# One value matmul for the high and low parts of the attention probabilities, with the second half of the bank copied by ScalarE and added by GpSimd

## The chip, the cores and the metric

The kernel runs on one core of a Trainium2 chip. The metric is the time of one execution on the device in microseconds (us). The kernel before takes 2233.69 us, the median of three runs (2232.92 to 2233.96).

Engines are named as in the profile: PE is the matrix engine (TensorE) and PEld its weight loads, DVE is VectorE, ACT is ScalarE, POOL is GpSimd, SP is the engine that issues the transfers. Each executes its own instructions in a fixed order and waits for others by semaphores.

## The reference

The reference is one layer of a decoder: a SwiGLU half block, two attention mixers side by side, a second SwiGLU half block and a gated input embedding, for 1024 tokens of width 1024 in float32. The change is inside the two mixers. Each has 8 heads of width 64:

```python
# forgetting attention, per block of queries
logits = jnp.einsum('bqhd,bkhd->bhqk', qi, k) * scale
logits = logits + Fq[..., None] - Fk          # running sums of log forget gates
w = jax.nn.softmax(jnp.where(mask, logits, -jnp.inf), axis=-1)
y = jnp.einsum('bhqk,bkhd->bqhd', w, v)

# stick-breaking attention, per block of queries (strictly causal)
z = jnp.einsum('bqhd,bkhd->bhqk', qi, k) * scale
log_1m = jnp.where(mask, jax.nn.log_sigmoid(-z), 0.0)
after = lax.cumsum(log_1m, axis=3, reverse=True) - log_1m
a = jnp.where(mask, jnp.exp(jax.nn.log_sigmoid(z) + after), 0.0)
y = jnp.einsum('bhqk,bkhd->bqhd', a, v)
```

In both, a triangular matrix of probabilities is multiplied with the values of the head. The change concerns this last product.

## The kernel before

Float32 accuracy is had from two rounded parts: a tensor is split into a high part (a cast to the matrix engine's rounded format, on ACT) and a low part (what the cast left over, on DVE or POOL), and products are made part by part. For the values, both parts of a head lie side by side in one weight tile of 128 columns: columns 0 to 63 hold the high part, 64 to 127 the low part (`v2[:, kb, hd, :]`, tile X). A product of that weight with probabilities therefore gives 128 rows: rows 0 to 63 are the high values' share, rows 64 to 127 the low values' share, and the two are added afterwards.

**Steps.** The attention loop runs over 16 heads, h = 0 to 7 forgetting and h = 8 to 15 stick-breaking, and in each over four blocks c = 0 to 3 of 256 queries. One such pair (h, c) is a step here. Block c sees the keys 0 to 256(c+1). `scores` of a step makes the two rows of its probabilities (row 0 and row 1, 128 queries each) in two T tiles, in the forgetting heads so: POOL adds the mask to the bias on the diagonal block (L981), PE makes the products (L990, L991), DVE adds the bias and takes the minimum (L995, first the part left of the diagonal, which reads the bias tile GF, then the diagonal, which reads what L981 wrote), ACT takes the exponential (L1001), DVE the reciprocal (L1002) and POOL scales (L1003). In the stick-breaking heads ACT takes two sigmoids (L998, L999), POOL masks the diagonal (L1005), DVE scans (L966) and POOL multiplies (L1013, L1017). There are four T buffers, so a step reuses the two tiles of the step before last.

`apply` works on the step before: for each pair of key blocks, from the diagonal pair down, PE turns the probabilities (transposes, L1042), ACT casts the high part (L1044), DVE makes the low part (L1045) into a tile PT with the two parts side by side (`pt[:, 0, :]` and `pt[:, 1, :]`), and PE multiplies with the values (L1065). The products of all pairs are summed in one bank `av` of the accumulator memory (PSUM), of which there is one buffer. At the end ACT copies rows 64 to 127 (L1084) and DVE adds rows 0 to 63 to them (L1085), which gives 64 rows of the tile Y for this head. In the diagonal pair the second key block meets only the second 128 queries, so there the widths are 256, 128, 128, 256; in other pairs four times 256. A group here is the value matmuls of one pair; there are 160, of which 64 are diagonal.

**What sets the order.** While a step's scores and products wait for other engines, PE works on fill: other matmuls of the layer (queries, keys and values of later heads, gates, branches), a share of which is woven in after every piece by `take`. The fill has work for other engines too: ACT casts weights (L136), POOL subtracts to get their low part (L146), and for a later pair of heads POOL takes a power (L850) and scales (L852) to normalise queries and keys. PE's order is written out by hand (`pe`), as is that of the L146 among themselves and, in the stick-breaking heads, that of the scans and of L1044 and L1045. The rest is ordered by a scheduler when the program is built. Some transposes of the fill (L882) use the `av` bank too.

## Time and profile before

| | |
|---|---|
| median of three runs | 2233.69 us |
| span of the profiled execution | 2230.9 us |
| PE busy | 2218.2 us (99%) |
| DVE, ACT, POOL busy | 1490.2, 972.1, 813.9 us |
| granted PE clock | 1.00 throughout |
| forgetting heads | about 733 to 1005 us |
| stick-breaking heads | about 1005 to 1372 us |
| value matmuls (L1065) | 640 |

The profile is of one execution, the runs of three others; the span runs from the first to the last instruction, and the profiled execution has no other time of its own. A row of a group reads: line, engine, operation, output<-input, shapes, count | busy us, mean ns of one | idle time before it and what ended it. A row of the timeline reads: start, length, engine, line, operation, shapes, count (rows that follow each other alike are merged), and in brackets the engine's idle time before it. The end of a matmul is modelled, and matmuls overlap, so the distance between the starts is what one costs.

### The profile page before, as it was taken

Reading aid. Unit: us, or ns where it says so; the run is one execution under the profiler, and the core shown is the slowest. Engines: PE = TensorE matmul, PEld = TensorE weight load, DVE = VectorE, ACT = ScalarE, POOL = GpSimd, SP = SyncE. Lnnn points to the kernel's source line nnn. Section 1 sums busy time; section 2 is a strip of 40 time slices with the busy share of each in tenths; the row PEclk is TensorE's granted clock in tenths of the full one; section 3 lists DMA queues with packets and bytes.
Section 4 is the critical chain, followed back from the end, with each engine's and each line's share of the span. In section 5 each row is a group of like instructions: output and inputs, shape, how many; then the busy total and the mean of one; then the engine's idle time right before and its main releaser. Section 6 shows DMA issues by size and latency. Waiting matters only on the chain.

```text
span 2230.9 us, 29212 instructions
## 1 busy us (share of the span) xinstructions
PE 2218.2 (99%) x10857; PEld 1864.3 (84%) x10857; DVE 1490.2 (67%) x2188; ACT 972.1 (44%) x1694; POOL 813.9 (36%) x709
## 2 busy tenths in 40 slices
PE   9999999999999999999999999999999999999999
PEld 7888888888889888888988888887888888888887
DVE  7855545497895565666666676799654555778873
ACT  6433333333454555555456564245333333434441
POOL 0344444310015466455456654400644443200111
PEclk9999999999999999999999999999999999999999
DMA  8232322474433133132124236731423232655132
GB/s 325 94 121 84 112 101 98 152 291 149 147 132 96 29 95 95 29 98 69 39 72 118 62 125 215 266 140 55 140 95 118 85 128 81 254 199 208 62 119 89
DMA packets 187710, 278.03 MB, mean 125 GB/s; under 512 B 27944, under 2 KB 110120, under 8 KB 187568
## 3 DMA queue, kind: packets, MB, share of 16 engines
q1 hardware_dynamic: 187568, 276.17, 36.7%
q8 instruction: 85, 1.39, 0.3%
q14 instruction: 57, 0.47, 0.1%
HBM read 192.47 MB, written 75.27 MB: 120 GB/s over the span
## 4 chain that ended last, share of the span: by engine, by line
PE 91%; DVE 4%; ACT 2%; issue 1%; DMA 1%; POOL 0%; SPq 0%; DVEq 0%; ACTq 0%; POOLq 0%
PE ps L496 36%; PE ps L388 19%; PE ps L763 11%; PE ps L755 7%; PE ps L1307 4%; PE ps L1662 4%; PE ps L1065 3%; PE ps L1042 2%; PE ps L449 2%; PE ps L991 1%; PE ps L990 1%; PE ps L1357 1%; DVE H L113 1%; ACT H L112 1%; ACT T L1001 0%
## 5 line engine op out<-in xcount | busy, mean ns | idle before, releaser
L388 PE MATMUL ps<-H,H 128*128 128x512 f32 x2184 | 497.3, 389 | 0.0
L388 PEld LDWEIGHTS ps<-H,H 128*128 128x128 f32 x2184 | 409.5, 188 | 85.0
L496 PE MATMUL ps<-H,WL 128*128 128x512 f32 x1008 | 238.9, 389 | 0.0
L496 PEld LDWEIGHTS ps<-H,WL 128*128 128x128 f32 x1008 | 189.2, 188 | 39.3
L763 PE MATMUL ps<-H,WH 128*128 128x512 f32 x640 | 176.1, 401 | 0.0
L1045 DVE TENSOR_TENSOR PT<-ps,PT 128x512 fp32r<-128x512 f32 (+1 forms) x160 | 100.6, 634 | 78.5 <-ACT PT L1044 77.6
L496 PE MATMUL ps<-H,Q 128*128 128x512 f32 x576 | 137.4, 389 | 0.0
L396 DVE SCALAR_TENSOR_TENSOR X<-ps,X 128x512 f32<-128x512 f32 x168 | 108.6, 682 | 41.8 <-PE ps L388 41.7
L763 PEld LDWEIGHTS ps<-H,WH 128*128 128x128 f32 x640 | 113.5, 188 | 18.4
L496 PEld LDWEIGHTS ps<-H,Q 128*128 128x128 f32 x576 | 108.1, 188 | 22.5
L1044 ACT CAST PT<-ps 128x512 fp32r<-128x512 f32 (+1 forms) x160 | 86.9, 549 | 85.0 <-PE ps L1042 81.1
L146 POOL TENSOR_TENSOR WL<-RAW,WH 128x512 fp32r<-128x512 f32 (+1 forms) x92 | 108.6, 1202 | 39.4 <-ACT WH L136 28.0
L496 PE MATMUL ps<-X,WL 128*128 128x512 f32 x480 | 115.6, 390 | 0.0
L209 POOL TENSOR_TENSOR PT<-PT,RN 128x1024 f32<-128x1024 f32 x2 | 4.8, 2413 | 295.0 <-ACT RN L203 295.0
L1065 PEld LDWEIGHTS ps<-PT,X 128*128 128x128 f32 x640 | 96.7, 189 | 18.9 <-DVE PT L1045 4.7
L755 PE MATMUL ps<-WH,H 128*128 128x256 f32 (+2 forms) x576 | 111.4, 323 | 0.2 <-DVE log_f L818 0.2
L1065 PE MATMUL ps<-PT,X 128*128 128x256 f32 (+1 forms) x640 | 105.7, 283 | 2.7 <-DVE PT L1045 1.4
L496 PEld LDWEIGHTS ps<-X,WL 128*128 128x128 f32 x480 | 89.9, 188 | 19.1 <-DVE WL L113 0.5
L1003 POOL TENSOR_TENSOR T<-T,l 128x128 f32<-128x128 f32 (+3 forms) x64 | 73.2, 1150 | 88.9 <-DVE l L1002 83.6
L496 PE MATMUL ps<-H,PT 128*128 128x512 f32 x432 | 103.2, 390 | 0.2 <-DVE PT L113 0.2
L283 POOL TENSOR_TENSOR PT<-GF,RN 128x512 f32<-128x512 f32 x20 | 33.2, 1658 | 174.1 <-DVE GF L539 89.9
L496 PEld LDWEIGHTS ps<-H,PT 128*128 128x128 f32 x432 | 80.8, 188 | 18.0 <-DVE PT L113 1.3
(418 smaller groups left out, 4810.8 us busy)
## 6 DMA issues: line engine op xcount, KB each, us to landing
hidden<-PT SPq DMA_DIRECT2D x40, 512.0 KB, 3.1
WH<-in_ffn_w_gate_dram SPq DMA_DIRECT2D x38, 512.0 KB, 5.4
Q<-hidden SPq DMA_DIRECT2D x24, 512.0 KB, 6.4
hidden<-RN SPq DMA_DIRECT2D x22, 512.0 KB, 2.6
KH<-in_ffn_w_up_dram SPq DMA_DIRECT2D x20, 512.0 KB, 6.2
KL<-in_ffn_w_up_dram SPq DMA_DIRECT2D x20, 512.0 KB, 6.9
T<-in_ffn_w_down_dram SPq DMA_DIRECT2D x20, 512.0 KB, 4.4
RAW<-in_w_in_dram SPq DMA_DIRECT2D x18, 512.0 KB, 4.3
```

The costliest lines, as they stand in the source:

```text
L146: ins = eng_lo.tensor_sub(lo[part], raw[part], f(hi[part]))
L388: pe(nc.tensor.matmul(groups[g][t][:], wt[:, b, k, t * P:(t + 1) * P], act[:, a, k, :], start=(fresh and n == 0), stop=(i in (6, 1, 4) and ...
L396: nc.vector.scalar_tensor_tensor(xs, groups[g][t][:], scale, xs, ALU.mult, ALU.add)
L496: pe(nc.tensor.matmul(ps[:], hl[:, a, k, :], rhs(m, b, k), start=(first and i == 0), stop=(final and i == 11), skip_group_check=True))
L755: pe(nc.tensor.matmul(ps[:, :n], hT[t // 4][a][:, k, (t % 4) * P:(t % 4 + 1) * P], w[k // d][b][:, k % d, :n], start=(i == 0), stop=(i == ...
L763: pe(nc.tensor.matmul(ps[:], w[a][:, k, :], hT[half][b][:, k, :], start=(i == 0), stop=(i == 23)))
L1003: nc.gpsimd.tensor_mul(T[:, :n], T[:, :n], l[:].broadcast_to([P, n]))
L1044: high = nc.scalar.copy(pt[:, 0, :width], ps[:, :width])
L1045: low = nc.vector.tensor_sub(pt[:, 1, :width], ps[:, :width], f(pt[:, 0, :width]))
L1065: pe(nc.tensor.matmul(o, lh, r, start=(kpair == c and i == 0), stop=(kpair == 0 and i == 3)))
L1307: pe(nc.tensor.matmul(ps[:], w[a][:, k, :], yT[g][b][:, k, half * 512:half * 512 + 512], start=(i == 0), stop=(i == 11)))
L1662: pe(nc.tensor.matmul(ps, pl["w"][d, k // 2][b][:, k % 2, m * P:(m + 1) * P], hT[half][a][:, k, cs], start=(i == 0), stop=(i == 23)))
```

## The change

Two matmuls in place of four make a pair's product. The moving operand of one is the high and the low part of the turned probabilities, twice 256 columns, and its output takes the whole bank of 512 columns: columns 0 to 255 hold the products of the high part, 256 to 511 those of the low part. For the second key block of the diagonal pair it is twice 128. So at the end of a step the bank has four quarters. The first two (rows 64 to 127 and 0 to 63 of the first half) are joined as before. Of the second half only rows 0 to 63 are used: ACT copies them to `part` (64x256), and POOL adds `part` to Y. The product of the low values with the low probabilities (rows 64 to 127), which was in the sum before, is left out of it. `part` lies in the second T tile of the step that is being finished.

```diff
         def values(kpair):
             pt = pts[kpair]
-            mm = []
-            for kb in (2 * kpair, 2 * kpair + 1):
-                for b in range(2):
-                    c0 = (kb % 2) * 256
-                    if kb < 2 * c + 1:
-                        mm.append((av[:, 0:256], v2[:, kb, hd, :], pt[:, b, c0:c0 + 256]))
-                    else:
-                        mm.append((av[:, P:256], v2[:, kb, hd, :], pt[:, b, c0:c0 + P]))
-            if kpair == c:
-                mm = [mm[0], mm[2], mm[3], mm[1]]
-            for i, (o, lh, r) in enumerate(mm):
-                pe(nc.tensor.matmul(o, lh, r, start=(kpair == c and i == 0), stop=(kpair == 0 and i == 3)))
+            both = av[:].rearrange("p (b n) -> p b n", b=2)
+            for i in range(2):
+                kb, c0 = 2 * kpair + i, 256 * i
+                q0 = 0 if kb < 2 * c + 1 else P
+                pe(nc.tensor.matmul(both[:, :, q0:256], v2[:, kb, hd, :], pt[:, :, c0:c0 + 256 - q0], start=(kpair == c and i == 0), stop=(kpair == 0 and i == 1)))
...
         ys = Y["t"][hh * HD:(hh + 1) * HD, c * 256:(c + 1) * 256]
+        part = step["pr"][1][hh * HD:(hh + 1) * HD, 0:256]
         nc.scalar.copy(ys, av[HD:P, :256])
         nc.vector.tensor_add(ys, av[0:HD, :256], ys)
+        nc.scalar.copy(part, av[0:HD, 256:512])
+        nc.gpsimd.tensor_add(ys, ys, part)
```

In the changed kernel the value matmul is L1058, the first copy and the DVE add are L1078 and L1079, the new copy and the POOL add L1080 and L1081; all lines above these are as before.

How the change moves instructions is shown at three places. The first is PE at a diagonal pair, its value matmuls and the transposes behind them; before:

```order
L1065 MATMUL ps_9228<-PT_9233,X_7472 128x256
L1065 MATMUL ps_9228<-PT_9233,X_7472 128x128 x2
L1065 MATMUL ps_9228<-PT_9233,X_7472 128x256
L1042 MATMUL ps_9262<-identf,T_9077 128x128
L1042 MATMUL ps_9262<-identf,T_9101 128x128
```

and now:

```order
L1058 MATMUL ps_9244<-PT_9249,X_7424 128x512
L1058 MATMUL ps_9244<-PT_9249,X_7424 128x2x128
L1042 MATMUL ps_9284<-identf,T_9082 128x128
L1042 MATMUL ps_9284<-identf,T_9106 128x128
L1042 MATMUL ps_9284<-identf,T_9082 128x128
```

Four matmuls have become two; everything else on PE keeps its place.

The second place is POOL in the steps (2,0) and (2,1), the first two of the third forgetting head; before:

```order
L981 TENSOR_TENSOR T_6316<-GF_5924,mask_fox 128x128
L981 TENSOR_TENSOR T_6339<-GF_5924,mask_fox 128x128
L850 TENSOR_TENSOR qkss_5592<-qkss_5592,mhalf 128x16
L852 TENSOR_TENSOR RN_5590<-RN_5590,qkss_5592 128x1024
L1003 TENSOR_TENSOR T_6316<-T_6316,l_6318 128x128
L1003 TENSOR_TENSOR T_6339<-T_6339,l_6341 128x256
L981 TENSOR_TENSOR T_6453<-GF_5924,mask_fox 128x128
L981 TENSOR_TENSOR T_6470<-GF_5924,mask_fox 128x128
L146 TENSOR_TENSOR WL_6426<-RAW_6327,WH_6424 128x512 x2
L146 TENSOR_TENSOR WL_6431<-RAW_6330,WH_6429 128x512 x2
```

and now:

```order
L981 TENSOR_TENSOR T_6298<-GF_5918,mask_fox 128x128
L1081 TENSOR_TENSOR Y_5575<-Y_5575,T_6116 64x256
L850 TENSOR_TENSOR qkss_5592<-qkss_5592,mhalf 128x16
L981 TENSOR_TENSOR T_6321<-GF_5918,mask_fox 128x128
L852 TENSOR_TENSOR RN_5590<-RN_5590,qkss_5592 128x1024
L1003 TENSOR_TENSOR T_6298<-T_6298,l_6300 128x128
L1003 TENSOR_TENSOR T_6321<-T_6321,l_6323 128x256
L981 TENSOR_TENSOR T_6429<-GF_5918,mask_fox 128x128
L146 TENSOR_TENSOR WL_6404<-RAW_6309,WH_6402 128x512 x2
L146 TENSOR_TENSOR WL_6409<-RAW_6312,WH_6407 128x512 x2
L1081 TENSOR_TENSOR Y_5575<-Y_5575,T_6215 64x256
L981 TENSOR_TENSOR T_6446<-GF_5918,mask_fox 128x128
```

The two L981 of a step stood next to each other ahead of the fill's POOL work. Now that of row 1 stands behind the add, and with it behind L850 in (2,0) and behind four L146 in (2,1).

The third place is POOL in the step (3,0); before:

```order
L146 TENSOR_TENSOR WL_6737<-RAW_6598,WH_6735 128x512 x2
L981 TENSOR_TENSOR T_6796<-GF_6314,mask_fox 128x128
L981 TENSOR_TENSOR T_6817<-GF_6314,mask_fox 128x128
L850 TENSOR_TENSOR qkss_6507<-qkss_6507,mhalf 128x16
L852 TENSOR_TENSOR RN_6505<-RN_6505,qkss_6507 128x1024
L1003 TENSOR_TENSOR T_6796<-T_6796,l_6798 128x128
```

and now:

```order
L981 TENSOR_TENSOR T_6766<-GF_6296,mask_fox 128x128
L146 TENSOR_TENSOR WL_6711<-RAW_6574,WH_6709 128x512 x2
L850 TENSOR_TENSOR qkss_6483<-qkss_6483,mhalf 128x16
L852 TENSOR_TENSOR RN_6481<-RN_6481,qkss_6483 128x1024
L1081 TENSOR_TENSOR Y_6295<-Y_6295,T_6532 64x256
L981 TENSOR_TENSOR T_6787<-GF_6296,mask_fox 128x128
L1003 TENSOR_TENSOR T_6766<-T_6766,l_6768 128x128
```

Here the add and the L981 of row 1 stand behind both L850 and L852. On DVE the order is unchanged: the L995 of row 1 stands ahead of the first L1045 of the step, as it did.

## The prediction

> **What bounds the kernel now.** I read the page's busy times and chain of waits first, then the stretches, the groups of instructions, and the timeline round the ends of the attention steps.

> ```profile
> span 2230.9 us, 29212 instructions
> PE 2218.2 (99%) x10857; PEld 1864.3 (84%) x10857; DVE 1490.2 (67%) x2188; ACT 972.1 (44%) x1694; POOL 813.9 (36%) x709
> PE 91%; DVE 4%; ACT 2%; issue 1%; DMA 1%; POOL 0%; SPq 0%; DVEq 0%; ACTq 0%; POOLq 0%
> ...
> 733.00:1005.00 272.00, 270.07 (x1589) 234.67 (x1588) 164.30 (x507) 148.49 (x319) 151.73 (x154) 1.00 0.25 69
> 1005.00:1372.00 367.00, 365.42 (x2058) 315.95 (x2057) 246.39 (x377) 209.72 (x433) 208.46 (x227) 1.00 0.32 95
> ```

> PE is busy 99% of the span and carries 91% of the chain. The last two rows are the stretches that the change touches, forgetting heads and then stick-breaking heads (length, then busy time of PE, weight loads, DVE, ACT, POOL, and the granted clock 1.00). PE stands idle under 2 us in each. So PE time removed comes off the end, and any new PE wait goes onto it: there is no idle time to swallow it. POOL is 56% busy in the first stretch, but what counts is what stands ahead of a given instruction in its queue.

> **The matmuls.** These groups and timeline rows price them.

> ```profile
> L1065 PE MATMUL ps<-PT,X 128*128 128x256 f32 x512 | 102.4, 290 | 1.9 <-DVE PT L1045 1.1 <-ACT PT L1044 0.6
> L1065 PE MATMUL ps<-PT,X 128*128 128x128 f32 x128 | 24.2, 255 | 0.8 <-DVE PT L1045 0.2
> ...
> 793.43 0.62 PE L755 MATMUL ps<-RAW,H 128*128 128x512 f32 x2
> 793.89 0.64 PE L1065 MATMUL ps<-PT,X 128*128 128x256 f32 x4
> ...
> 799.75 0.62 PE L1065 MATMUL ps<-PT,X 128*128 128x256 f32 x4
> 800.21 0.60 PE L1042 MATMUL ps<-identf,T 128*128 128x128 f32 x4
> ...
> 839.26 0.64 PE L1065 MATMUL ps<-PT,X 128*128 128x256 f32 x4
> 839.74 0.60 PE L1042 MATMUL ps<-identf,T 128*128 128x128 f32 x4
> ```

> Since matmuls overlap, I take the distance between starts. Two 512-column matmuls take 793.89 - 793.43 = 0.46, 0.23 each. A full group (four of 256) takes 0.48, 0.12 each. A diagonal group (256, 128, 128, 256) takes 0.46 as well, so a 128-column one costs (0.46 - 0.24)/2 = 0.11, nearly as much as 256: below 256 columns it is no longer the columns that set the pace. After the change a full group is 2 x 0.23 = 0.46 and a diagonal one 0.23 + 0.12 = 0.35. The 640 matmuls are 160 groups, 64 diagonal and 96 full: 64 x 0.11 + 96 x 0.015 = 8.5 us at most.

> A matmul now reads high and low part at once, so the group cannot start on the high part while DVE finishes the low one. Comparing the start of each L1065 group with the end of its L1045, 23 of the 160 start before it. Those lose most of the gain, and full ones some 0.1 us each beside it: I take **-5.4 us** (-8.5 to -3). That the moving operand is now two runs of 256 rather than one is shown by no row; it is bounded by 0 and by the four-matmul price, a gain of 0.

> [...]

> **The new copy and add.** Each of the 64 steps gets an ACT copy of 64x256 and a POOL add of 64x256.

> ```profile
> L1084 ACT COPY Y<-ps 64x256 f32<-64x256 f32 x64 | 23.6, 369 | 71.8 <-PE ps L1065 70.7
> L1085 DVE TENSOR_TENSOR Y<-ps,Y 64x256 f32<-64x256 f32 x64 | 26.6, 415 | 47.2 <-ACT Y L1084 45.9
> L1003 POOL TENSOR_TENSOR T<-T,l 128x256 f32<-128x256 f32 x7 | 4.3, 617 | 0.1
> L1017 POOL TENSOR_TENSOR T<-T,RN 128x256 f32<-128x256 f32 x16 | 12.9, 806 | 0.0
> L1013 POOL TENSOR_TENSOR T<-T,RN 128x255 f32<-128x255 f32 x16 | 15.3, 955 | 19.2 <-DVE RN L966 19.1
> L981 POOL TENSOR_TENSOR T<-GF,mask_fox 128x128 f32<-128x128 f32 x60 | 26.5, 463 | 16.9 <-PE ps L1042 16.0 <-POOL T L1003 0.8
> L850 POOL TENSOR_TENSOR qkss<-qkss,mhalf 128x16 f32<-128x16 f32 x6 | 17.5, 2914 | 18.8 <-DVE qkss L849 18.6
> L852 POOL TENSOR_TENSOR RN<-RN,qkss 128x1024 f32<-128x1024 f32 x6 | 11.4, 1907 | 0.5
> L882 PE MATMUL ps<-identf,RN 128*128 128x128 f32 x56 | 8.5, 273 | 0.5 <-DVE Y L1085 0.5
> ```

> The copy is the L1084 copy, 0.37. The add has two full operands of 256 columns like L1017, 0.81; with a broadcast operand it would be 0.62, beside DVE scans 0.96. I take 0.81. Both engines have the time (64 x 0.81 = 52 us on POOL over 639). What counts is order: `part` lies in the second T tile of the step just applied, so that tile comes free after the POOL add and no longer after its last transpose. The next user, row 1 of the step being scored, waits: L981 on POOL, the first L995 on DVE, L998/L999 on ACT. DVE and ACT run in order, and behind the stalled L995 or L1001 stand L1044 and L1045 of the same step, which the value matmuls need.

> The order listing shows that in the forgetting heads the add often stands behind long POOL work. Worked in full for step (3,0), where it stands behind L850 and L852:

> ```profile
> 833.04 2.91 POOL L850 TENSOR_TENSOR qkss<-qkss,mhalf 128x16 f32<-128x16 f32 x1
> 834.55 0.35 DVE L995 CUSTOM_DVE_ANT_0 T<-T,ps,m 128x128 f32<-128x128 f32 x1
> 834.94 0.51 ACT L1001 ACTIVATE T<-T,m 128x256 f32<-128x256 f32 x1 [0.93 <-DVE m L995]
> 835.57 0.48 ACT L1044 CAST PT<-ps 128x384 fp32r<-128x384 f32 x1
> 836.03 1.91 POOL L852 TENSOR_TENSOR RN<-RN,qkss 128x1024 f32<-128x1024 f32 x1
> 836.08 0.56 DVE L1045 TENSOR_TENSOR PT<-ps,PT 128x384 fp32r<-128x384 f32 x1 [0.34 <-ACT PT L1044]
> 837.28 0.63 PE L1065 MATMUL ps<-PT,X 128*128 128x256 f32 x4
> ```

> L852 ends at 837.94, the add at 838.75, L981 (0.46) at 839.2. The diagonal L995 starts at 839.25 for 834.55, 4.7 late. L1001, L1044 and L1045 follow each other without slack, so the low part is ready at 836.64 + 4.7 = 841.35, and the value matmuls of 837.28 stall **4.1 us**.

> Two other patterns: in (2,0) the add comes in time but L981 stands behind L850; in (2,1) the add stands behind four L146.

> ```profile
> 794.96 0.42 DVE L1085 TENSOR_TENSOR Y<-ps,Y 64x256 f32<-64x256 f32 x1
> 796.20 2.91 POOL L850 TENSOR_TENSOR qkss<-qkss,mhalf 128x16 f32<-128x16 f32 x1 [3.24 <-DVE qkss L849]
> 796.72 0.35 DVE L995 CUSTOM_DVE_ANT_0 T<-T,ps,m 128x128 f32<-128x128 f32 x1
> 798.10 0.56 DVE L1045 TENSOR_TENSOR PT<-ps,PT 128x384 fp32r<-128x384 f32 x1 [0.20 <-ACT PT L1044]
> ...
> 805.36 5.05 POOL L146 TENSOR_TENSOR WL<-RAW,WH 128x512 fp32r<-128x512 f32 x4 [1.41 <-ACT WH L136]
> 808.55 0.55 DVE L995 CUSTOM_DVE_ANT_0 T<-GF,ps 128x384 f32<-128x384 f32 x1 [0.35 <-PE ps L991]
> 811.01 0.56 DVE L1045 TENSOR_TENSOR PT<-ps,PT 128x384 fp32r<-128x384 f32 x1 [0.34 <-ACT PT L1044]
> 811.57 0.63 PE L1065 MATMUL ps<-PT,X 128*128 128x256 f32 x4
> ```

> (2,0): L1085 ends at 795.38, the part copy some 0.6 later (L845 stands ahead of it on ACT), so add at 796.0 to 796.8, L850 to 799.7, L981 to 800.2; L995 3.5 late, the low part at 798.66 + 3.5 = 802.15 against a group at 799.75: **2.4 us**. (2,1): L146 ends at 810.41, add at 811.2; L995 2.7 late, no slack at 811.57: **2.7 us**. The same arithmetic on the other forgetting steps gives about 2.4 in (5,0), (6,0) and (3,2), 2.8 in (6,1), 1.9 in (7,0), 1.5 in (7,3), 1.4 in (3,3) and (6,2), 1.2 in (4,0), 0.6 in (7,2), 0.4 in (1,1) and (5,1), 0.3 in (3,1), nothing elsewhere: **+28 us** in all; with an add of 0.62 it is 25, of 0.96 it is 31. After a stall POOL's backlog could be shorter, since PE then starts the next step later: if every second stall of a run of neighbours vanished, 20 would be left.

> Stick-breaking heads: there the add stands behind row 0's work only.

> ```profile
> 1237.67 0.40 ACT L999 ACTIVATE T<-ps 128x256 f32<-128x256 f32 x1
> 1238.05 0.46 POOL L1013 TENSOR_TENSOR T<-T,RN 128x127 f32<-128x127 f32 x1
> 1238.90 0.28 PE L1065 MATMUL ps<-PT,X 128*128 128x256 f32 x1
> ```

> In (13,0) the add ends at 1238.51 + 0.8 = 1239.3; L999 of row 1, which stood at 1237.67, is 1.7 late, with L1044 behind it and a group at 1238.90 that has no slack: 1.7 us. Over these heads the same sum gives **+4 us** (3 to 5).

> The `av` bank comes free after the part copy, 0.37 later. L882 is the only one that already waits there (0.5 us now); at four places its slack is under 0.37: **+1 us**. SP only loses a few places in its order; its next Y store waits for one more add, and nothing waits for that. The very last add lies beside some 11 us of branch matmuls.

> Sum: 2230.9 - 5.4 + 28 + 4 + 1 = 2258.5 of span. The median of the runs (2233.69) is 2.8 above the span, so about **2260 us**.

> [...]

> **Rivals.**

> 1. *Forecast: POOL's queue decides*, 2245 to 2277. For it: PE's idle share and the three worked steps.
> 2. *No change.* The scheduler's positions hold, but the queue is short when the add arrives; then each step has only the chain copy, add, copy, POOL add. The same arithmetic with an idle POOL gives about +4 over the forgetting heads; with -5.4 + 4 + 1 that is about the same as before, near 2234. Against it: L850 alone takes 2.9 us.
> 3. *Faster.* The slack covers the lateness entirely: 119 of the 160 groups have over 0.4 us between the end of L1045 and the group's start. PE's gain stands alone, -5.4 to -8.5: 2225 to 2228. It decides if the part copy and add end before row 1's first L995, 1 to 3 us after the step's last value matmul. In about half of the steps they do; it would have to be nearly all.
> 4. *Worse.* The L146 that stand behind an add come late as well and the fill matmuls wait for their weights: 0.81 in each of some 15 steps, +12, about 2272. Or two runs of 256 cost as much as four matmuls, and the gain is nil: +5, 2265. Against both: none of the PE rows above waits for POOL now, and weights are split a step or more ahead of their use.

> **Chances.** 1: 0.62. 4: 0.20. 2: 0.10. 3: 0.08. A change within 0.2% (4.5 us) cannot be told from none here. Faster 0.08, same 0.10, slower 0.82. The range takes case 1, most of case 4 and the upper edge of 2: 2236 to 2277; the forecast's own is 2245 to 2277.

> **What would show it.** 256 value matmuls of 512 columns and 64 of 2x128, groups of 0.46 and 0.35 between starts; POOL adds near 0.8; the stretch of the forgetting heads longer by 20 to 28 us at the same PE work, with PE's idle time charged to L1045 and L1044, most in (3,0) and heads 2, 3, 5, 6 and 7; DVE's L995 or POOL's L981 waiting for POOL. Wrong would be: PE idle still under 5 us in both stretches, or a stall at steps where POOL was free.

## The result, and the profile after

The changed kernel takes 2274.88 us (median of four runs, 2274.28 to 2275.44) against 2233.38 us in the runs beside it: 1.0186 times as long, 95% interval 1.0171 to 1.0200. It is slower by 41.5 us, where 26 were forecast. The profile is of the execution of 2275.44 us.

The page of the changed kernel, first its span, PE's busy row and the chain of waits:

```profile
span 2273.7 us, 28587 instructions
PE 2228.6 (98%) x10537; PEld 1851.2 (81%) x10537; DVE 1497.4 (66%) x2188; ACT 990.8 (44%) x1758; POOL 864.4 (38%) x773
PE 82%; DVE 7%; ACT 4%; POOL 3%; issue 3%; DMA 1%; SPq 0%; POOLq 0%; DVEq 0%; ACTq 0%
```

PE's part of the chain fell from 91% to 82%, and POOL, which had none, has 3%. PE has 320 matmuls fewer and is nevertheless busy 10 us longer (2228.6 against 2218.2). That is the first sign of something the prediction had not reckoned with.

The two stretches of attention (length, then busy time of PE, weight loads, DVE, ACT, POOL, then the granted clock):

```profile
734.00:1037.00 303.00, 278.73 (x1442) 232.18 (x1442) 163.62 (x505) 155.05 (x344) 171.98 (x180) 0.96 0.23 62
1037.00:1413.30 376.30, 363.48 (x1872) 302.47 (x1871) 251.35 (x375) 220.03 (x466) 237.60 (x261) 1.00 0.31 91
```

The forgetting heads take 32 us longer (303 for 271), the stick-breaking heads 11 us (376 for 365); the rest of the program is as before to 0.2 us. PE is idle 24 us in the first stretch and 13 in the second, 1.9 and 1.6 before. And the granted clock of the first stretch is 0.96.

The matmuls, the new copy and the POOL add, by groups:

```profile
L1058 PE MATMUL ps<-PT,X 128*128 128x512 f32 x256 | 91.9, 420 | 35.7 <-DVE PT L1045 35.3
L1058 PE MATMUL ps<-PT,X 128*128 128x256 f32 x64 | 18.7, 292 | 0.0
L1081 POOL TENSOR_TENSOR Y<-Y,T 64x256 f32<-64x256 f32 x64 | 51.1, 799 | 70.5 <-ACT T L1080 61.0 <-PE ps L755 5.6 <-PE ps L763 2.4
L1080 ACT COPY T<-ps 64x256 f32<-64x256 f32 x64 | 23.4, 365 | 23.1 <-DVE Y L1079 22.5
```

The add takes 0.80 us, the copy 0.37, as estimated. PE's idle time stands almost wholly ahead of L1058, charged to the low part, L1045. Why L1045 is late the list of waits says (who waited for whom: us in total, times, longest):

```profile
DVE T L995 <- POOL Y L1081: 22.3, 16, 4.2
ACT T L999 <- POOL Y L1081: 16.0, 17, 2.9
DVE T L995 <- POOL T L981: 12.2, 8, 3.1
```

Row 1 of the scores waits for its T tile, on DVE in the forgetting heads and on ACT in the others. A step's name here is that of the step being scored; its value matmuls are those of the step before. The timeline of (3,0), which the prediction worked out in full:

```profile
839.97 2.91 POOL L850 TENSOR_TENSOR qkss<-qkss,mhalf 128x16 f32<-128x16 f32 x1 [0.48 <-DVE qkss L849]
842.96 1.90 POOL L852 TENSOR_TENSOR RN<-RN,qkss 128x1024 f32<-128x1024 f32 x1
844.82 0.71 POOL L1081 TENSOR_TENSOR Y<-Y,T 64x256 f32<-64x256 f32 x1
845.57 0.29 DVE L995 CUSTOM_DVE_ANT_0 T<-GF,ps 128x128 f32<-128x128 f32 x1 [4.24 <-POOL Y L1081]
845.62 0.45 POOL L981 TENSOR_TENSOR T<-GF,mask_fox 128x128 f32<-128x128 f32 x1
847.49 0.56 DVE L1045 TENSOR_TENSOR PT<-ps,PT 128x384 fp32r<-128x384 f32 x1 [0.20 <-ACT PT L1044]
848.10 0.62 PE L1058 MATMUL ps<-PT,X 128*128 128x512 f32 x2 [3.43 <-DVE PT L1045]
```

L850, L852, the add, L981, then DVE, ACT, DVE and at last PE, which has stood idle for 3.43 us. The chain is the predicted one, link by link; 4.1 us was the estimate. What comes behind it was not predicted. Four stretches of one us, the second and third just after this stall:

```profile
847.00:848.00 1.00, 0.00 (x0) 0.00 (x0) 0.67 (x3) 1.00 (x5) 0.61 (x1) 1.00 0.02 8
...
850.00:851.00 1.00, 1.00 (x6) 0.90 (x5) 0.50 (x1) 0.00 (x0) 0.00 (x0) 0.50 0.06 16
851.00:852.00 1.00, 1.00 (x6) 0.80 (x5) 0.00 (x0) 0.00 (x0) 0.00 (x0) 0.50 0.00 0
...
853.00:854.00 1.00, 1.00 (x9) 0.96 (x8) 0.97 (x2) 0.65 (x2) 0.00 (x0) 1.00 0.00 0
```

While PE stands idle the clock still reads 1.00 here. Some 1.5 us after it has started again the granted clock falls to 0.50, where PE has 6 matmuls in a stretch of one us for 9 behind it; after 3.41 us it is 1.00 again. There are seven such drops, after the stalls of 2.33, 3.43, 2.75, 2.13, 2.41, 3.93 and 2.44 us; six last 3.41 us and the one after 2.75 twice that. The stall of 2.43 us at 800.5 was followed by none, nor were those of 1.75 and 1.39.

What sets the one of 2.43 us apart shows in the places of the drops. They start at 818.83, 849.55, 870.03, 941.71, 982.67, 999.74 and 1276.22 us, and all the distances are whole multiples of 3.413 us (9, 6, 21, 12, 5 and 81 of them). So in this trace the drops lie on a beat of 3.413 us that does not start anew with a stall. Cut along this beat, the stalls of 2.43 us (the first three rows) and of 2.33 us (the last two) look like this:

```profile
798.35:801.76 3.41, 2.14 (x12) 1.44 (x10) 0.36 (x2) 0.45 (x2) 3.41 (x3) 1.00 0.00 0
801.76:805.18 3.42, 2.26 (x15) 2.00 (x16) 1.90 (x4) 1.59 (x5) 1.91 (x3) 1.00 0.02 5
805.18:808.59 3.41, 3.41 (x19) 2.65 (x17) 1.90 (x4) 3.15 (x5) 0.53 (x2) 1.00 0.17 38
...
815.42:818.83 3.41, 1.51 (x10) 1.47 (x11) 1.92 (x8) 1.55 (x4) 1.97 (x3) 1.00 1.01 295
818.83:822.24 3.41, 3.41 (x16) 3.41 (x15) 1.44 (x8) 2.51 (x5) 1.18 (x2) 0.50 0.60 228
```

The first stall lies across two beats, in which PE is idle for 1.27 and 1.16 us, and the next beat is at full clock. The second puts 1.90 us of idleness into one beat, and the next is at half clock. The other six drops follow beats with 1.96 to 3.41 us of idleness; among the beats without a drop behind them the largest idleness is 1.75 us.

The run of the matmuls alone (below) has the same 10537 PE matmuls in the same order and no drop before the program's end. Against its distances from start to start, the drops of the change cost **12.7 us**. By an estimate from their length, eight beats at half clock are 13.6 us of full-speed work (8 x 3.41 / 2), but at the start of three of them PE was still idle (0.68, 0.08 and 0.39 us). The four runs had a mean clock of 0.994 to 0.996; one beat at half clock takes 0.0008 off that mean (1.7 of 2274 us), so by this estimate not all had the same number of drops.

### The profile page after: what moved, and what is told of

It reads as the page before. It is cut to its first block, busy times and chain, and to the rows that moved or that the text cites. A ratio compares the mean times of both kernels' runs of the same rounds, so it can differ in the third digit from the quotient of the medians.

```text
span 2273.7 us, 28587 instructions
## 1 busy us (share of the span) xinstructions
PE 2228.6 (98%) x10537; PEld 1851.2 (81%) x10537; DVE 1497.4 (66%) x2188; ACT 990.8 (44%) x1758; POOL 864.4 (38%) x773
## 4 chain that ended last, share of the span: by engine, by line
PE 82%; DVE 7%; ACT 4%; POOL 3%; issue 3%; DMA 1%; SPq 0%; POOLq 0%; DVEq 0%; ACTq 0%
PE ps L496 35%; PE ps L388 18%; PE ps L763 6%; PE ps L755 6%; PE ps L1658 4%; PE ps L1303 3%; PE ps L1058 3%; PE ps L449 2%; PE ps L1042 2%; POOL WL L146 1%; PE ps L1353 1%; PE ps L991 1%; PE ps L990 1%; DVE PT L1045 1%; DVE H L113 1%
## 5 line engine op out<-in xcount | busy, mean ns | idle before, releaser
L1045 DVE TENSOR_TENSOR PT<-ps,PT 128x512 fp32r<-128x512 f32 (+1 forms) x160 | 100.0, 633 | 73.0 <-ACT PT L1044 72.1
L1058 PE MATMUL ps<-PT,X 128*128 128x512 f32 x320 | 99.9, 394 | 35.7 <-DVE PT L1045 35.3
L146 POOL TENSOR_TENSOR WL<-RAW,WH 128x512 fp32r<-128x512 f32 (+1 forms) x92 | 104.9, 1161 | 37.3 <-ACT WH L136 32.7
L1044 ACT CAST PT<-ps 128x512 fp32r<-128x512 f32 (+1 forms) x160 | 85.5, 546 | 67.2 <-PE ps L1042 66.2
L755 PE MATMUL ps<-WH,H 128*128 128x256 f32 (+2 forms) x576 | 112.0, 325 | 0.2 <-DVE log_f L818 0.2
L1058 PEld LDWEIGHTS ps<-PT,X 128*128 128x128 f32 x320 | 56.4, 193 | 62.1 <-DVE PT L1045 54.1
L966 DVE TENSOR_TENSOR_SCAN RN<-GF,RN 128x127 f32<-128x127 f32 (+2 forms) x96 | 96.6, 1007 | 2.8
```

Source lines behind the costliest of these rows:

```text
L146: ins = eng_lo.tensor_sub(lo[part], raw[part], f(hi[part]))
L755: pe(nc.tensor.matmul(ps[:, :n], hT[t // 4][a][:, k, (t % 4) * P:(t % 4 + 1) * P], w[k // d][b][:, k % d, :n], start=(i == 0), stop=(i == ...
L966: order("dve", nc.vector.tensor_tensor_scan(*args))
L1044: high = nc.scalar.copy(pt[:, 0, :width], ps[:, :width])
L1045: low = nc.vector.tensor_sub(pt[:, 1, :width], ps[:, :width], f(pt[:, 0, :width]))
L1058: pe(nc.tensor.matmul(both[:, :, q0:256], v2[:, kb, hd, :], pt[:, :, c0:c0 + 256 - q0], start=(kpair == c and i == 0), stop=(kpair == 0 an ...
```

## The experiments

The theory after the result: the T tile, held past its transposes for the new part, makes row 1 of the next scores late; POOL's queue turns that into stalls of microseconds; and long stalls cost clock on top (the tile theory). Two rivals: the merged matmul stalls for its own sake, because it needs the low part before it can start (the matmul theory); or the added work on ACT and POOL makes both late in whatever buffer the part lies (the load theory). Each median stands beside that of runs of the kernel before on the same chip; those medians are 2233.05 to 2233.26 us.

### The matmuls alone

```diff
-        part = step["pr"][1][hh * HD:(hh + 1) * HD, 0:256]
         nc.scalar.copy(ys, av[HD:P, :256])
         nc.vector.tensor_add(ys, av[0:HD, :256], ys)
-        nc.scalar.copy(part, av[0:HD, 256:512])
-        nc.gpsimd.tensor_add(ys, ys, part)
```

> The two matmuls per pair alone: neither the new copy nor the POOL add is made, so the share of the low probabilities is left out of the result. This prices the matmul side by itself. Tile and load theory: 4 to 8 us faster than before, 2225 to 2229 us, granted clock 1.00 throughout. Matmul theory: 2260 to 2275.

Measured: 2229.84 us, 0.9986 of before (0.9976 to 0.9995), 0.8 us above what the tile and the load theory gave. Its busy times, and behind them what PE waited for (us in total, times, longest):

```profile
PE 2211.3 (99%) x10537; PEld 1842.0 (83%) x10537; DVE 1489.1 (67%) x2188; ACT 971.5 (44%) x1694; POOL 813.7 (37%) x709
...
PE ps L1058 <- DVE PT L1045: 6.4, 15, 1.2
PE ps L882 <- DVE Y L1078: 1.9, 2, 1.4
```

The matmul theory falls: the merge makes the kernel 3.2 us faster. PE's idle time in attention rose from 3.5 to 8.9 us, so the matmuls themselves save 8.6 us (3.2 + 5.4), the 8.5 of the prediction's upper bound, and waits for the low part take most of it back.

### The copy and the add alone

```diff
+        part = step["pr"][1][hh * HD:(hh + 1) * HD, 0:256]
+        nc.scalar.copy(part, av[0:HD, 0:256])
+        nc.gpsimd.tensor_add(ys, ys, part)
```

added to the kernel before, with its four matmuls.

> The four matmuls of before, and beside them the new copy and POOL add with the part in the T tile (the part is copied from rows 0 to 63 of the first half, so those are added twice). Tile theory: all the cost and none of the gain, 2265 to 2282 us. Matmul theory: 2232 to 2238, as before. Load theory: 2255 to 2275.

Measured: 2276.56 us, 1.0194 of before (1.0178 to 1.0210): the whole loss, without the merged matmul, as the tile theory had it and 1.6 us above the upper end of the load theory. Its value matmuls now wait, where they had waited for 2.7 us in all:

```profile
L1065 PE MATMUL ps<-PT,X 128*128 128x256 f32 x512 | 106.9, 298 | 23.7 <-ACT PT L1044 21.5 <-DVE PT L1045 1.9
```

Here PE waits for the high part instead of the low one, since this group may start on the high part. Both stand behind row 1 in their queues, which fits the loss being much the same. The granted clock is 0.96 in the forgetting heads (734 to 1037 us) and 1.00 in the others, as with the change.

### The part in a buffer of its own

```diff
-        part = step["pr"][1][hh * HD:(hh + 1) * HD, 0:256]
+        part = stat([P, 256], "part", 1)[hh * HD:(hh + 1) * HD, :]
```

and, to make room, the size 1088 of the buffers RAW, WH, WL and Y set to 1056.

> The part lies in a buffer of its own (64x256, one buffer) and no longer in the step's second T tile; copy, POOL add and matmuls stay. Tile theory (T comes free only behind the POOL add, so row 1 of the next scores is late, PE stalls, and long stalls cost clock): the 33 us of added PE idle and the 14 us of clock go, 2226 to 2236 us. Matmul theory (a group of two matmuls cannot start before the low part and stalls by itself): 2265 to 2275, as the whole change. Load theory (52 us more on POOL and 23 us more on ACT make both late, in whatever buffer): 2250 to 2270.

Measured: 2251.71 us (1.0081; 1.0063 to 1.0100). That is 16 us above the tile theory's upper end and inside what the load theory gave, although the clock is 1.00. But the stretches tell of another cause: before and behind attention, where no instruction was changed, it takes 4.7 and 7.7 us longer. One group of the first 700 us shows it, before and here:

```profile
L496 PE MATMUL ps<-H,WL 128*128 128x512 f32 x504 | 119.4, 389 | 0.0
```

```profile
L496 PE MATMUL ps<-H,WL 128*128 128x512 f32 x504 | 121.7, 393 | 0.0
```

These matmuls take their weights from a WL tile. Such matmuls became slower with the new size and make up 9 of the 12 us (sums of the distances between starts, against the run of the matmuls alone); the rest is spread over others, by under 1 us each. So 12 us of this run are the buffers' layout, and the next run leaves the layout as it was. Its part is rounded to bfloat16, which takes half the bytes:

```diff
-        part = step["pr"][1][hh * HD:(hh + 1) * HD, 0:256]
+        part = st.tile([P, 256], mybir.dt.bfloat16, tag="part", bufs=1, name=nm("part"))[hh * HD:(hh + 1) * HD, :]
```

> Copy and POOL add as in the change, the part in a buffer of its own that fits without making other buffers smaller (bfloat16, 512 bytes a partition). In e1_own the stretches outside attention, where nothing was changed but buffer sizes, were 12 us longer; here they should be as before, 734 and 856 us. Tile theory: 2231 to 2238 us. Load theory: 2245 to 2255.

Measured: 2239.54 us, 1.0030 of before (1.0018 to 1.0041), between the two forecasts and nearer to the tile theory. Up to the first value matmul and from the last one on it takes 734.1 and 860.8 us, as before (734.2 and 860.8). The profile is of the fastest of its six executions, 2237.21 us, without a clock drop; the slowest, 2241.60 us, had a mean clock of 0.998. Inside attention:

```profile
734.00:1006.60 272.60, 266.26 (x1443) 223.48 (x1442) 163.62 (x506) 156.28 (x344) 169.35 (x180) 1.00 0.25 69
1006.60:1375.00 368.40, 360.88 (x1873) 301.45 (x1872) 249.54 (x375) 219.69 (x466) 237.52 (x260) 1.00 0.32 94
```

In the forgetting heads (first row) PE is idle 6.3 us, as with the matmuls alone: there the tile explains the whole loss. In the stick-breaking heads it is idle 7.5 us against 2.7 with the matmuls alone and 12.8 with the change. So there the load theory has its share: some 4.8 us come from the copy on ACT and the add on POOL although the tile is free, 5.3 from the tile. The one buffer is not what costs instead: no copy into it waits for the add before. Which of copy and add makes the 4.8 us was not taken apart.

### The tile or POOL's add

```diff
-        nc.gpsimd.tensor_add(ys, ys, part)
+        nc.vector.tensor_add(ys, ys, part)
```

> The change, but the last add on DVE and not on POOL; the part still lies in the T tile. This separates POOL's queue from the tile. If the queue is the cause (the add and L981 stand behind L850, L852 and L146), the tile comes free about 1.3 us after the first DVE add, which most steps can bear: 2231 to 2240 us, clock 1.00. If holding the T tile past its transposes is enough by itself: 2250 to 2275.

Measured: 2258.46 us, 1.0114 of before (1.0099 to 1.0130). Neither forecast named the mechanism, which the timeline of step (3,0) shows:

```profile
836.73 0.42 DVE L1081 TENSOR_TENSOR Y<-Y,T 64x256 f32<-64x256 f32 x1 [0.28 <-ACT T L1080]
836.80 3.12 POOL L850 TENSOR_TENSOR qkss<-qkss,mhalf 128x16 f32<-128x16 f32 x1
840.00 1.90 POOL L852 TENSOR_TENSOR RN<-RN,qkss 128x1024 f32<-128x1024 f32 x1
841.86 0.45 POOL L981 TENSOR_TENSOR T<-GF,mask_fox 128x128 f32<-128x128 f32 x1
842.35 0.35 DVE L995 CUSTOM_DVE_ANT_0 T<-T,ps,m 128x128 f32<-128x128 f32 x1 [4.76 <-POOL T L981]
844.41 1.01 PE L1058 MATMUL ps<-PT,X 128*128 128x512 f32 x2 [3.63 <-DVE PT L1045]
```

The last add is now done by DVE in good time, at 837.15. But L981, the mask add of row 1, can only start after it, and L850 and L852 now stand ahead of it in POOL's order. PE stalls for 3.63 us without any new instruction on POOL. So the forgetting heads stall without an add on POOL too: PE is idle there for 19.6 us, against 24.3 with the change and 6.3 with the matmuls alone. That the tile is held some microseconds past its transposes, and L981 has thereby lost its place ahead of the fill's POOL work, is enough for most of it. The added DVE work is not the cause: with a second DVE add and no tile held (under "Versions without the tile") PE is idle there for 9.0 us. With the add on POOL it is worse by 16 us, since the add too waits in that queue: PE is idle for 9.6 us more in both stretches together, and eight beats run at half clock instead of four.

If so, it must help to give L981 its place back and keep tile, copy and POOL add. In the next version both mask adds of a forgetting step are issued first and the waiting L850 and L852 (`norm`) behind them. The POOL add then no longer stands behind L850 and L852 either, so this run does not tell the two apart; the one before does.

```diff
+            for i in (2 * step["c"], 2 * step["c"] + 1):
+                Ts[i] = slot("T", [P, S])
+                mask = nc.gpsimd.tensor_add(Ts[i][:, i * P:(i + 1) * P], step["fb"]["t"][:, i * P:(i + 1) * P], mask_fox[:])
...
+            for norm in last["defer"]:
+                norm()
```

> The whole change, part in the T tile and add on POOL, with one thing moved: the fill's power and scaling (L850, L852) are issued behind both mask adds (L981) of the next forgetting step, so neither the POOL add nor L981 stands behind them. The L146 stay where they are. If what costs is that the held T tile drops L981 behind POOL's long work, the stalls of the steps whose add or L981 stood behind L850 (2.4, 3.4, 2.8, 2.1 and 2.4 us in this change) shrink to under 1 us each, five or six of the eight clock drops go with them, and it takes 2250 to 2260 us; the stalls behind L146 stay. If the held tile costs by itself, wherever L981 stands: 2268 to 2276.

Measured: 2260.49 us, 1.0123 of before (1.0109 to 1.0137): 14.4 us less than the change, half a microsecond above the range that was expected. Of the five stalls behind L850 four are gone and the fifth is 0.7 us; those behind L146 stay (2.33 and 3.62 us), as expected. Two others of 2.0 and 2.1 us appear, in (4,0) at the value matmuls and somewhat later at the transposes L882; the first of these was 0.7 and the second 0.08 in the change. They brought clock drops of their own, so that four beats at half clock are left of eight where two or three were expected. A queue that is put right at one place passes some of the wait on.

### The clock

In front of the groups that stall for over 2 us stand matmuls that wait for nothing, 88 in all; their result is overwritten by the group's first matmul.

```diff
+        def idle_work(n):
+            for _ in range(n):
+                pe(nc.tensor.matmul(av[:].rearrange("p (a b) -> p a b", a=4), v2[:, 0, hd, :], v2[:, 0:4, hd, :], start=True, stop=True))
...
```

> The whole change, and in the eight longest stalls (2.1 to 3.9 us) 8 to 16 matmuls of 512 columns are put ahead of the waiting group; they wait for nothing and their result is overwritten. They remove no wait, they only keep PE busy during it. If the halved clock after these stalls comes from PE's idleness, it stays 1.00 and 11 to 14 us come back: 2260 to 2265 us. If the clock falls for another reason (load, time, a neighbour), 2274 to 2278.

Measured: 2265.42 us, 1.0144 of before (1.0128 to 1.0160), 9.5 us less than the change, just outside what was expected. The two stretches, cut at the same instructions as those of the change:

```profile
734.00:1028.20 294.20, 286.93 (x1521) 237.58 (x1520) 163.66 (x506) 154.97 (x344) 172.34 (x180) 1.00 0.23 64
1028.20:1403.40 375.20, 364.41 (x1883) 302.80 (x1882) 251.18 (x375) 219.90 (x467) 237.82 (x261) 1.00 0.31 91
```

The granted clock is 1.00 in both stretches, where the first had 0.96 in the change, and PE is idle there for 7.3 us instead of 24.3; no wait was removed, and more work for PE made the kernel faster. That the drops of this kernel come from PE's idleness is thereby shown. Why 9.5 us came back and not 12.7 was not taken apart; 88 matmuls of 0.23 us are 20 us, nearly as long as the stalls that they fill, and where they last past a stall they cost time themselves.

### Versions without the tile

The bank's second half can go into Y by a second DVE add, without copy, scratch or POOL:

```diff
-        nc.scalar.copy(part, av[0:HD, 256:512])
-        nc.gpsimd.tensor_add(ys, ys, part)
+        nc.vector.tensor_add(ys, av[0:HD, 256:512], ys)
```

> No copy, no POOL add, no scratch: DVE adds the bank's second half straight into Y (64x256 from the bank, like the first DVE add, 0.42 us, 64 times). The merged matmuls alone took 2229.8. Tile theory: no T tile is held, PE has no new long wait; the DVE adds lie in DVE's gaps but for a few steps where the low part comes later, 2230 to 2235 us, clock 1.00. Load theory (any extra work in the step's tail costs): 2240 to 2256.

Measured: 2235.14 us, 1.0010 of before (1.0001 to 1.0019): no stall of over 1.6 us, but 5.3 us above the matmuls alone. PE's idle time in attention is 2.5 us higher, which is nearly all at L882 (4.2 us for 1.9). Of the 4.2 us, 3.0 end with the second DVE add, one DVE add later than the `av` bank came free before, and 1.2 with POOL's L852.

```diff
+            split = step["hc"] + (kpair,) in {(1, 2, 2), (1, 3, 0), (3, 2, 0), (5, 2, 2), (5, 3, 0), (6, 2, 0), (7, 2, 2), (12, 2, 1), (0, 1, 1), (6, 1, 1)}
+            bs = (slice(0, 1), slice(1, 2)) if split else (slice(0, 2),)
...
+            for i, b in ((i, b) for b in bs for i in range(2)):
...
```

> As the version with the DVE add straight from the bank, and in ten groups whose low part comes late the two products are made apart again, high part first (four matmuls, 0.46 to 0.48 us). If the matmul side loses 3 to 5 us to waits for the low part, as PE's idle time in the merged version says (8.9 us in attention against 3.5 before), 1.5 to 3.5 us come back against the version without the split: 2227 to 2233 us. If those waits are made up elsewhere, no difference.

Measured: 2233.86 us, 1.0005 of before (0.9996 to 1.0014): 1.3 us less than without the split, a little under the forecast; the intervals of the two runs overlap, so that a gain is not shown. L882 then had 5.7 us of waits, so its bank was changed:

```diff
-                        run(fst(x, "sc" if calls[0] else "av")[half][1])
+                        run(fst(x, "sc" if calls[0] else "pt")[half][1])
```

> The version with the DVE add from the bank and ten split groups (2233.9 us), and the fill's transposes L882 that wrote the av bank write a bank of the turning transposes instead. In that version PE stalls six times at L882, 5.6 us in all, because the av bank comes free one DVE add later. If that is all that is left to gain, 2228 to 2231 us; if the transposes now wait for a bank of the other kind, 2232 to 2236.

> The same with a bank of the scores. Three of those exist and a step with over 512 keys takes two per row, so row 1 can wait for the transposes: 2229 to 2236 us. Against the other version it tells which bank has room.

Measured: 2234.97 us with the bank of the transposes (1.0009; 1.0001 to 1.0018) and 2232.10 with that of the scores (0.9996; 0.9987 to 1.0005). In the first PE now waits at the transposes L1042, in the second at L990; the wait has moved on. The last run took for each place the bank with less idle time and split three more groups:

```diff
+                        run(fst(x, "sc" if calls[0] or c == 2 else "av")[half][1])
```

> The version with the DVE add from the bank, with the fill's transposes L882 in a bank of the scores where c is 2 and in the av bank where c is 3 (at each place the bank at which PE stood idle for less time in the two versions before), and three more groups split into high part first. PE's idle time in attention was 9.5 us with the scores' bank everywhere; 1.9 us of it at places with c = 3 and some 0.7 us at the three groups should go: 2229 to 2231 us, 2 to 4 us less than before, which the repeated runs can tell from none. If each wait that goes is paid elsewhere, 2232 as without.

Measured: 2231.84 us, 0.9995 of before (0.9986 to 1.0004). That is the best version that sums all that the change sums, and it cannot be told from the kernel before, nor from the run before it (0.3 us). The 2229 to 2231 us that were to be had if the waits went did not come: each wait that went was largely paid elsewhere.

## Why the prediction was right, and where it was not

The direction, the place and the chain were right; the size was 41.5 us for 26. Against the spans of the profiled executions (42.8 us more), with the run of the matmuls alone as the dividing line, by the prediction's terms:

| term | forecast | measured | from |
|---|---|---|---|
| matmuls, with their waits for the low part | -5.4 | -2.4 | span of the matmuls alone, 2228.5 for 2230.9 |
| forgetting heads, PE stalls | +28 | +18.0 | PE idle 24.3 against 6.3 with the matmuls alone |
| stick-breaking heads, PE stalls | +4 | +10.2 | PE idle 12.8 against 2.7 |
| `av` bank | +1 | in the two rows above | |
| granted clock | 0 | +12.7 | distances between matmul starts in the drops, against the matmuls alone |
| matmuls next to a wait | 0 | +4.3 | the same distances elsewhere |

The last row is no idle time of PE in the profile: where a group waits, the matmul before the wait and the first one behind it take some 0.16 and 0.10 us more from start to start than where nothing waits.

- **The matmuls.** The bound of 8.5 was met (8.6 saved), and the rates were as taken: 0.23 us for 512 columns. The term was set too high by 3 us, since the waits for the low part cost 5.4 us and not 3.1.
- **The price of the copy and the add** was right: 0.37 and 0.80 us for 0.37 and 0.81. The 0.96 that the prediction gives for an add beside DVE scans is the mean of the L1013 rows; that the scans are the reason is not shown. In the profile of before these L1013 of 255 columns run beside L966 for 28% of their time, the L1017 of 256 columns, with 0.81, for 45%.
- **The forgetting heads.** The three steps worked out in full came to 2.43, 2.33 and 3.43 us for 2.4, 2.7 and 4.1. With (3,2), (5,0), (6,0) and (6,1) the seven longest came to 19.4 us for 19.2. What did not come are the other 9 us: everywhere else in these heads PE is idle for 4.8 us, less than the 6.3 with the matmuls alone. (3,3) and (6,2) were to stall 1.4 us each and did not stall at all; (7,0) stalled 0.5 us for 1.9. For the first two, each behind a long stall, the caution that the prediction named fits, since POOL works on meanwhile; for the others no run shows the reason.
- **The cause inside POOL.** The prediction had both the add and L981 behind L850 and L146 and spoke of the add's lateness first. The version with the add on DVE shows that L981's place alone makes most of the stalls, 13 of the 18 us.
- **The stick-breaking heads** were mis-sized, 10.2 for 4. The forecast counted row 1's wait for the tile; the run with a buffer of its own shows that about half comes from the copy and the add themselves, which the prediction had at nothing there ("Both engines have the time").
- **The clock** is the step that was missing. The prediction counted a stall at its own length. After seven of the stalls of over 2 us the granted clock was 0.50 for 3.41 us or twice that, which makes nearly a third of the loss (12.7 of 41.5 us). In the trace of before there is no stall of that length inside attention, the longest being 0.57 us, and the clock is 1.00 there, so no row could have priced it.
- **Some of it was luck.** With every term at the upper end of its own bounds (-3, 31, 5 and 1) the sum is 2265 us of span and 2268 of time. The measured 2275 lies above that, in the part of the range that was there for the fourth case. Without the clock's 12.7 us it would have been 2262, close to the 2260 of the forecast; but that closeness too comes from errors that offset each other, 10 us too much in the forgetting heads against 6 too little in the others, 3 at the matmuls and 4 next to the waits.

Of the rivals, "no change" and "faster" fell with the result. "Worse" came nearest in size (2265 and 2272 us) but had not the cause: in attention no PE matmul or weight load is released by the L146 on POOL, and the merged matmuls gained what the rates say.

## What to carry to other kernels

Scratch that is borrowed from a rotating buffer moves the moment at which that buffer comes free to the last engine that reads the scratch, and with it the place of the buffer's next user in every queue that a scheduler orders; here that place, more than the 0.8 us of the add, made 13 of the 18 us of stalls in the forgetting heads. Where the matrix engine is busy 99% of the time, ask of every added instruction what waits for the tile that it touches, and look behind every stall for the clock as well: here seven of the eight over 2 us (2.13 to 3.93) were followed by a beat of 3.41 us at a clock of 0.50 or by two, by estimate up to 1.7 us a beat (half of 3.41) in addition to the stall's own length. The gain of a merged operation is to be set against what its parts could do early: two matmuls that need high and low part together saved 8.6 us and lost 5.4 to waiting for the low part.
